# ConvFFN up and gate as seven block products instead of eight, and the down projection as a phase of its own

## The chip, the cores and the metric

The kernel runs on one core of a Trainium2 chip. The metric is the device time of one execution in microseconds. Its engines are TensorE (PE; PEld is its weight load), VectorE (DVE), ScalarE (ACT), GpSimd (POOL) and SyncE (SP), which issues nearly all transfers.

## The reference

One layer of a streaming encoder over 1024 prompt tokens and 32 sample tokens (1056 columns), in float32. Three mixers come first and are not touched. The part that changes is the ConvFFN (D_MODEL 1024, D_FF 2816):

```python
x = x + jnp.einsum('ble,ed->bld', jnp.concatenate([y_a, y_b, y_c], axis=-1), w_out)

h2 = _rmsnorm(x, norm_ffn_g)
up, gate = jnp.split(jnp.einsum('bld,df->blf', h2, w_up), 2, axis=-1)
g_conv, new_f = _causal_dwconv(gate, st_f, conv_ffn_w)
x = x + jnp.einsum('blf,fd->bld', jax.nn.silu(g_conv) * up, w_down)
```

Then a final RMSNorm. The convolution has 3 taps along the tokens; the last 2 gate inputs of each stream are outputs too.

## The kernel before, in words

Features lie on the 128 partitions and tokens along the columns, in three chunks `CH` of 256, 384 and 416. Each product is float32 by three matmuls (`three`, L245 to L250): weights and activations are split into a rounded part and its remainder (hi and lo, H and L), and hi·H, hi·L and lo·H are summed in PSUM. `convert` splits a weight block of 128x1024 with one ScalarE copy (L205) and one VectorE subtraction (L200); `weights` loads and converts a block or two ahead.

`o2`, the second half of the output projection, makes the residual stream `res` and the operands `fH`, `fL` of the ConvFFN in its evacuation `e_o2` (L1165 to L1176); behind its last block `rms_factor` (L1022 to L1024) makes the factor `rf` of each token, chunk by chunk. The ConvFFN runs over 22 feature blocks f in 11 pairs. For each f, `up_group` does the gate (8 row blocks x 3 chunks x 3 matmuls), its convolution and silu (L285, L290, L1203, L1205) and the up product, whose evacuation (L1211) multiplies; `mH` and `mL` (L1218, L1219) are the middle row in two parts and stay on chip. `down_group` adds the products of the pair before (8 output blocks x 3 chunks) into `res` (L1236 to L1240). The last two pairs go together, by chunks, with the last norm (`final`, `final_half`) among them. GpSimd does only `put_state` and `take_state` there (L475 to L483). No order is written out by hand: the order within an engine comes from a scheduler at build time, and each engine works through its own row of instructions in that order, waiting at each for what it needs.

## Time and profile before

| | us |
|---|---|
| median of 3 runs (1555.2 to 1558.69) | 1556.51 |
| span of the profiled execution | 1557.1 |
| PE busy in it | 1532.8 |
| DVE / ACT / POOL busy in it | 970.5 / 467.5 / 88.3 |
| from the first matmul of the ConvFFN (774.98) to the end | 782.1 |

A page of the profile lists busy time by engine, the chain of work that ended last, and the costliest groups of instructions. A matmul's own duration contains the pipeline; what each costs in a row of them is the distance of their starts.

### The profile page before, as it was taken

What the parts mean: (1) busy time and instruction counts of PE and PEld (TensorE: products, weight loads), DVE (VectorE), ACT (ScalarE), POOL (GpSimd) and SP (SyncE); (2) the same over time, 40 slices, a digit from 0 to 9 for tenths busy, and PEclk for the clock granted to TensorE, in tenths of its full rate; (3) what the DMA queues carried; (4) which work ended last, traced back from release to release, by engine and by line L of the source; (5) the groups of instructions that cost most, each with busy time, mean ns of one, the idle gap of its engine ahead of it and who ended that gap; (6) DMA issues with size and microseconds to landing.
All of it is one profiled execution on the core that took longest, in us unless ns stands there. A gap on an engine that the chain in (4) does not pass through costs nothing.

```text
span 1557.1 us, 23101 instructions
## 1 busy us (share of the span) xinstructions
PE 1532.8 (98%) x9677; PEld 1502.3 (96%) x9677; DVE 970.5 (62%) x1397; ACT 467.5 (30%) x754; POOL 88.3 (6%) x213
## 2 busy tenths in 40 slices
...
PEclk9999999999999999999999999999999999999999
...
GB/s 175 205 28 109 16 55 45 79 41 41 87 114 100 138 221 187 163 188 55 70 40 41 55 41 41 55 41 55 41 41 41 55 41 55 41 41 55 41 15 112
DMA packets 156758, 119.42 MB, mean 77 GB/s; under 512 B 9045, under 2 KB 145135, under 8 KB 156655
## 3 DMA queue, kind: packets, MB, share of 16 engines
...
q14 instruction: 27, 0.22, 0.0%
q10 hardware_dynamic: 16, 0.00, 0.0%
...
## 4 chain that ended last, share of the span: by engine, by line
PE 62%; DMA 1%; DVE 0%; ACT 0%; issue 0%; POOL 0%; SPq 0%; DVEq 0%; ACTq 0%; POOLq 0%
PE g L250 12%; PE g L245 12%; PE g L249 12%; PE g L1238 4%; PE g L1236 4%; PE g L1237 4%; PE xT L250 3%; PE xT L249 3%; PE xT L245 3%; PE xT L1236 1%; PE xT L1238 1%; PE xT L1237 1%; DMA zr<-zd 0%; DMA E<-acd 0%; PE yd L893 0%; PE st L883 0%
## 5 line engine op out<-in xcount | busy, mean ns | idle before, releaser
L245 PE MATMUL g<-hH,hi 128*128 128x416 f32 (+2 forms) x952 | 309.7, 325 | 0.0
L250 PE MATMUL g<-hH,lo 128*128 128x416 f32 (+2 forms) x952 | 307.3, 323 | 0.0
L249 PE MATMUL g<-hL,hi 128*128 128x416 f32 (+2 forms) x952 | 307.3, 323 | 0.0
L249 PE MATMUL g<-fL,hi 128*128 128x384 f32 (+2 forms) x792 | 255.9, 323 | 0.0
L250 PE MATMUL g<-fH,lo 128*128 128x384 f32 (+2 forms) x792 | 255.6, 323 | 0.0
L245 PE MATMUL g<-fH,hi 128*128 128x384 f32 (+2 forms) x792 | 255.6, 323 | 0.0
L245 PEld LDWEIGHTS g<-hH,hi 128*128 128x128 f32 x952 | 179.8, 189 | 1.8 <-issue 1.2
L249 PEld LDWEIGHTS g<-hL,hi 128*128 128x128 f32 x952 | 179.8, 189 | 0.4
L250 PEld LDWEIGHTS g<-hH,lo 128*128 128x128 f32 x952 | 179.6, 189 | 0.5 <-DVE lo L200 0.2
L290 DVE SCALAR_TENSOR_TENSOR cacc<-cb,par,cacc 128x1086 f32<-128x1086 f32 (+1 forms) x120 | 159.2, 1327 | 7.3 <-ACT cacc L287 5.7
L200 DVE TENSOR_TENSOR lo<-raw,hi 128x1024 fp32r<-128x1024 f32 x122 | 149.2, 1223 | 21.0 <-ACT hi L205 20.9
L249 PEld LDWEIGHTS g<-fL,hi 128*128 128x128 f32 x792 | 149.4, 189 | 0.4 <-issue 0.2
L250 PEld LDWEIGHTS g<-fH,lo 128*128 128x128 f32 x792 | 149.4, 189 | 0.5 <-issue 0.2
L245 PEld LDWEIGHTS g<-fH,hi 128*128 128x128 f32 x792 | 149.4, 189 | 0.3
L285 ACT ACTIVATE ca<-gb,par 128x1058 f32<-128x1058 f32 x22 | 26.0, 1182 | 407.8 <-DVE gb L1198 407.8
L1240 DVE TENSOR_TENSOR res<-res,g 128x416 f32<-128x416 f32 (+2 forms) x186 | 96.2, 522 | 60.7 <-PE g L1238 54.4
L1236 PE MATMUL g<-mH,hi 128*128 128x384 f32 (+2 forms) x396 | 129.0, 326 | 0.0
L1238 PE MATMUL g<-mH,lo 128*128 128x384 f32 (+2 forms) x396 | 128.5, 324 | 0.0
L1237 PE MATMUL g<-mL,hi 128*128 128x384 f32 (+2 forms) x396 | 128.0, 323 | 0.0
L205 ACT ACTIVATE hi<-raw 128x1024 fp32r<-128x1024 f32 x121 | 124.3, 1046 | 11.4 <-DMA raw<-in_w_in_dram 6.7
L1198 DVE TENSOR_TENSOR gb<-g,rf 128x384 f32<-128x384 f32 (+2 forms) x77 | 29.7, 410 | 142.4 <-PE g L250 142.4
L250 PE MATMUL xT<-fH,lo 128*128 128x256 f32 (+2 forms) x264 | 85.1, 323 | 0.0
...
## 6 DMA issues: line engine op xcount, KB each, us to landing
...
```

What stands on the lines that cost most here:

```text
L200: v.tensor_tensor(out=lo, in0=r, in1=hi.bitcast(F32), op=ALU.subtract)
L205: act.activation(hi, r, AF.Copy)
L245: pe.matmul(o, hi[:, k, :], x, start=first, stop=False)
L249: pe.matmul(o, hi[:, k, :], y, start=False, stop=False)
L250: pe.matmul(o, lo[:, k, :], x, start=False, stop=last)
L285: act.activation(out[:, u:u + n], buf[:, b:b + n], AF.Copy, scale=w_of(0))
L290: v.scalar_tensor_tensor(out=out[:, u:u + n], in0=buf[:, b + j:b + j + n], scalar=w_of(j), in1=out[:, u:u + n], op0=ALU.mult, op1=ALU.add)
L1198: v.tensor_tensor(out=buf[:, b:b + n], in0=ps[:, o:o + n], in1=rf[:, c0 + o:c0 + o + n], op=ALU.mult)
L1236: pe.matmul(o, hi[:, m, :], a[:, c0:c0 + w], start=(f == some[0]), stop=False)
L1237: pe.matmul(o, hi[:, m, :], b[:, c0:c0 + w], start=False, stop=False)
L1238: pe.matmul(o, lo[:, m, :], a[:, c0:c0 + w], start=False, stop=(f == some[-1]))
L1240: v.tensor_tensor(out=rc, in0=rc, in1=o, op=ALU.add)
```

## The change

Up and gate of one f, with the tokens halved (528 columns) and the 1024 input rows halved, are a 2 x 2 block product. One level of Strassen's scheme replaces its 8 block products by 7 (P1, P5, P6, P2, P7, P3, P4 in this order), each of 4 row blocks and two runs of 264 columns. Its operands are sums of weight halves (`make_sums`, on GpSimd), split again into two parts for each product (`make_w`), and sums of activation halves (`make_x`), made once at the start out of `rows` (the normalized residual before its factor), and split too (`split_x`). Sums of products are made in PSUM where a bank can go on, else in the evacuations (`after`): ScalarE copies P1, P5 and P2 out, GpSimd adds P1 and P5, VectorE adds for P6, P7, P3 and P4, and GpSimd multiplies by `rf`. `finish` does the convolution, the silu and the product, and writes the middle row to DRAM (`midd`). The residual stream is written to DRAM (`r2d`) by the evacuation of `o2`, and is loaded again for down.

The down projection comes after all f. For two halves h of the outputs and three chunks it adds over all 22 f in four PSUM banks: the same 1584 matmuls of 256, 384 and 416 columns as before. `next_wd` loads and splits down weights (in the first and third chunk of h = 0), `next_mid` loads and splits 128 rows of a chunk's middle from DRAM, both four f ahead. All of PSUM is one pool of eight banks. `up_group`, `down_group`, `fH`, `fL` and the resident `res` go; their removed lines are those of the kernel above and are not repeated:

```diff
+            x = rows[m] = slot(T, name=f"row{m}")
...
+            def e_o2(j, c0, w, ps, m=m, r=r, x=x):
...
-                act.activation(a[:, c0:c0 + w], rc, AF.Copy, scale=gk)
-                v.scalar_tensor_tensor(out=b[:, c0:c0 + w], in0=rc, scalar=gk,
-                                       in1=a[:, c0:c0 + w].bitcast(F32), op0=ALU.mult, op1=ALU.subtract)
+                act.activation(x[:, c0:c0 + w], rc, AF.Copy, scale=pcol(at["gf"] + m))
...
+                if j == 2:
+                    deferred.append(lambda: dma(out=r2d[m], in_=r))
...
+        def split_x(i, k, src):
+            q = (xpool.tile([P, T], F32R, name=f"X{i}{k}") if i == "P1" else slot(T, F32R, name=f"X{i}{k}"))
+            X[i, k] = q
+            act.activation(q[:, 0:H], src, AF.Copy)
+            v.tensor_tensor(out=q[:, H:T], in0=src, in1=q[:, 0:H].bitcast(F32), op=ALU.subtract)
+        def make_x(i, k):
+            a, b = rows[k], rows[k + 4]
+            b11, b12, b21, b22 = a[:, 0:H], a[:, H:T], b[:, 0:H], b[:, H:T]
+            if i == "P5":
+                t = xt_[k, 0] = slot(T, name="xt12")
+                pool.tensor_tensor(out=t[:, 0:H], in0=b12, in1=b11, op=ALU.subtract)
+                v.tensor_tensor(out=t[:, H:T], in0=b22, in1=t[:, 0:H], op=ALU.subtract)
+            if i == "P7":
+                t = xt_[k, 1] = slot(T, name="xt34")
+                pool.tensor_tensor(out=t[:, 0:H], in0=b22, in1=b12, op=ALU.subtract)
+                v.tensor_tensor(out=t[:, H:T], in0=b21, in1=xt_[k, 0][:, H:T], op=ALU.subtract)
+            src = {"P1": b11, "P2": b21, "P3": b22}.get(i)
+            if src is None:
+                n, h = {"P5": (0, 0), "P6": (0, 1), "P7": (1, 0), "P4": (1, 1)}[i]
+                src = xt_[k, n][:, h * H:h * H + H]
+            split_x(i, k, src)
+        raws, sums, wops = {}, {}, {}
...
+        def make_sums(f):
...
+            u, g = raws[f]
+            a, b = slot(1024, name="s12"), slot(1024, name="s34")
+            pool.tensor_tensor(out=a[:, 0:512], in0=g[:, 0:512], in1=g[:, 512:1024], op=ALU.add)
+            pool.tensor_tensor(out=a[:, 512:1024], in0=a[:, 0:512], in1=u[:, 0:512], op=ALU.subtract)
+            pool.tensor_tensor(out=b[:, 0:512], in0=u[:, 0:512], in1=g[:, 0:512], op=ALU.subtract)
+            pool.tensor_tensor(out=b[:, 512:1024], in0=u[:, 512:1024], in1=a[:, 512:1024], op=ALU.subtract)
+            sums[f] = (a, b)
...
+        def make_w(f, i):
...
+            n, h = {"P1": (0, 0), "P2": (0, 1), "P4": (1, 1), "P5": (2, 0), "P6": (2, 1), "P7": (3, 0),
+                    "P3": (3, 1)}[i]
+            src = (*raws[f], *sums[f])[n][:, 512 * h:512 * h + 512]
+            w = wops[f, i] = slot(1024, F32R, name="wop")
+            act.activation(w[:, 0:512], src, AF.Copy)
+            v.tensor_tensor(out=w[:, 512:1024], in0=src, in1=w[:, 0:512].bitcast(F32), op=ALU.subtract)
...
+            def product(self, i):
+                b = {"P1": "B", "P2": "B", "P5": "D", "P3": "D"}.get(i, "A")
+                new = i in ("P1", "P5", "P6")
+                w = wops.pop((self.f, i))
+                for c, (c0, n) in enumerate(C2):
+                    if new:
+                        self.banks[b, c] = bank()
+                    o = self.banks[b, c][:, 0:n]
+                    for k in range(4):
+                        hi, lo = w[:, k * P:k * P + P], w[:, 512 + k * P:512 + k * P + P]
+                        x = X[i, k]
+                        xh, xl = x[:, c0:c0 + n], x[:, H + c0:H + c0 + n]
+                        kw = {"skip_group_check": not new}
+                        pe.matmul(o, hi, xh, start=(new and k == 0), stop=False, **kw)
+                        pe.matmul(o, hi, xl, start=False, stop=False, **kw)
+                        pe.matmul(o, lo, xh, start=False, stop=(k == 3), **kw)
+                    self.after(i, c, c0, n, o)
...
+            def after(self, i, c, c0, n, o):
+                s1, s5 = self.s[:, c0:c0 + n], self.s[:, H + c0:H + c0 + n]
+                u2, s15 = self.t[:, c0:c0 + n], self.t[:, H + c0:H + c0 + n]
+                if i == "P1":
+                    act.activation(s1, o, AF.Copy)
+                elif i == "P5":
+                    act.activation(s5, o, AF.Copy)
+                    pool.tensor_tensor(out=s15, in0=s1, in1=s5, op=ALU.add)
+                elif i == "P6":
+                    v.tensor_tensor(out=u2, in0=o, in1=s1, op=ALU.add)
+                elif i == "P2":
+                    act.activation(self.u[:, c0:c0 + n], o, AF.Copy)
+                elif i == "P7":
+                    self.gate_to(H + c0, n, o, s15)
+                    if c == 1:
+                        pool.tensor_tensor(out=self.gb[:, 2 + H:2 + NP], in0=self.gb[:, 2 + H:2 + NP],
+                                           in1=rf[:, H:NP], op=ALU.mult)
+                        pool.tensor_tensor(out=self.gb[:, 4 + NP:4 + T], in0=self.gb[:, 4 + NP:4 + T],
+                                           in1=rf[:, NP:T], op=ALU.mult)
+                elif i == "P3":
+                    v.tensor_tensor(out=self.u[:, H + c0:H + c0 + n], in0=o, in1=u2, op=ALU.add)
+                    if c == 1:
+                        pool.tensor_tensor(out=self.u, in0=self.u, in1=rf, op=ALU.mult)
+                else:
+                    self.gate_to(c0, n, o, s1)
+                    if c == 1:
+                        pool.tensor_tensor(out=self.gb[:, 2:2 + H], in0=self.gb[:, 2:2 + H], in1=rf[:, 0:H],
+                                           op=ALU.mult)
+                        self.finish()
+            def finish(self):
+                f, gb, u = self.f, self.gb, self.u
+                take_state(fpack, gb, 2, f)
...
+                for _ in conv_steps(ca, 2, lambda i: pcol(at["w_f"] + NF * i + f), whole(gb, 2)):
+                    pass
+                act.activation(ca, ca, AF.Silu)
+                for t, a, n in run_pieces(2):
+                    v.tensor_tensor(out=u[:, t:t + n], in0=ca[:, a:a + n], in1=u[:, t:t + n], op=ALU.mult)
+                dma(out=midd[f], in_=u)
...
+        load_up(0)
+        load_up(1)
+        make_sums(0)
+        for i in ORDER:
+            for k in range(4):
+                make_x(i, k)
+            if i in ORDER[:3]:
+                make_w(0, i)
+        rows.clear()
+        xt_.clear()
...
+        AHEADW = 3
+        for n, (f, i) in enumerate(steps):
+            if i == ORDER[0]:
+                unit = Unit(f)
+                put_state(unit.gb, 2, "st_f", f, NF)
+            if i == ORDER[2] and f + 1 < NF:
+                make_sums(f + 1)
+            if n + AHEADW < len(steps):
+                make_w(*steps[n + AHEADW])
+            unit.product(i)
+            if i == ORDER[4]:
+                raws.pop(f)
+                sums.pop(f)
+                load_up(f + 2)
...
+        w_jobs = iter([(h, f) for h in range(2) for f in range(NF)])
+        CORDER = ((0, 1, 2), (2, 1, 0))
+        m_jobs = iter([(h, j, f) for h in range(2) for j in CORDER[h] for f in range(NF)])
+        def next_wd():
+            for h, f in w_jobs:
+                r = slot(512, name="rawd")
+                dma(out=r, in_=w_down[0, f * P:(f + 1) * P, 512 * h:512 * h + 512])
+                w = wd[h, f] = slot(1024, F32R, name="wd")
+                act.activation(w[:, 0:512], r, AF.Copy)
+                v.tensor_tensor(out=w[:, 512:1024], in0=r, in1=w[:, 0:512].bitcast(F32), op=ALU.subtract)
+                return
...
+        def next_mid():
+            for h, j, f in m_jobs:
+                r = small("midr")
+                dma(out=r[:, 0:w], in_=midd[f][:, c0:c0 + w])
...
+        for _ in range(4):
+            next_wd()
+            next_mid()
+        for h in range(2):
+            for m in range(4 * h, 4 * h + 4):
+                load_res(m)
...
+            for n, j in enumerate(CORDER[h]):
+                c0, w = CH[j]
...
+                ps = [bank() for _ in range(4)]
+                for f in range(NF):
+                    if h == 0 and n != 1:
+                        next_wd()
+                    next_mid()
+                    q = wd[h, f]
+                    a, b = mids.pop((h, j, f))
+                    for m in range(4):
+                        o = ps[m][:, 0:w]
+                        hi, lo = q[:, m * P:m * P + P], q[:, 512 + m * P:512 + m * P + P]
+                        pe.matmul(o, hi, a[:, 0:w], start=(f == 0), stop=False)
+                        pe.matmul(o, hi, b[:, 0:w], start=False, stop=False)
+                        pe.matmul(o, lo, a[:, 0:w], start=False, stop=(f == NF - 1))
+                    if n == 2:
+                        del wd[h, f], q
+                for m in range(4):
+                    rc = res[4 * h + m][:, c0:c0 + w]
+                    v.tensor_tensor(out=rc, in0=rc, in1=ps[m][:, 0:w], op=ALU.add)
+                if h and j:
+                    final(j)
+        final_half(1)
```

TensorE at the end of o2. Before, the matmul for the root mean square of the last chunk (`misc`, which waits for VectorE) stands 40 matmuls into the gate of f = 0:

```order
L245 MATMUL g_7368<-fH5_6993,hi57_7213 128x384
L1022 MATMUL misc_7326<-ss2_6450,ones_71 128x416 [waits DVE_49]
L249 MATMUL g_7368<-fL5_6994,hi57_7213 128x384
L250 MATMUL g_7368<-fH5_6993,lo57_7214 128x384
L245 MATMUL g_7368<-fH6_7102,hi57_7213 128x384
```

Now:

```order
L233 MATMUL g_7264<-gH7_6430,lo56_7091 128x416
L1005 MATMUL misc_7296<-ss2_6455,ones_71 128x416 [waits DVE_49]
L1272 MATMUL g_7472<-XP10_7346,wop_7358 128x264
L1273 MATMUL g_7472<-XP10_7346,wop_7358 128x264
L1274 MATMUL g_7472<-XP10_7346,wop_7358 128x264
```

It stands directly behind the last matmul of o2 and ahead of all of P1.

VectorE at the same place, now (`ss2` is the sum that this matmul reads, `xt12` a sum of activation halves that waits for GpSimd, `XP5` and the like are operands, `wop` a weight operand):

```order
L1152 TENSOR_TENSOR o2_7289<-g_7264,rb_6434 128x416 [waits PE_49]
L1206 TENSOR_TENSOR xt12_7361<-row4_6879,xt12_7361 128x528 [waits Pool_49]
L1154 TENSOR_TENSOR r1_7087<-r1_7087,o2_7289 128x416 [waits DVE_49]
L1197 TENSOR_TENSOR XP50_7364<-xt12_7361,XP50_7364 128x528 [waits Activation_49]
L1206 TENSOR_TENSOR xt12_7367<-row5_6985,xt12_7367 128x528 [waits Pool_49]
L1161 TENSOR_TENSOR ss2_6455<-ss2_6455,o2q_7293 128x416 [waits Activation_49]
...
L1197 TENSOR_TENSOR XP42_7457<-xt34_7427,XP42_7457 128x528 [waits Activation_49]
L1197 TENSOR_TENSOR XP43_7460<-xt34_7433,XP43_7460 128x528 [waits Activation_49]
L1247 TENSOR_TENSOR wop_7469<-rawf_7332,wop_7469 128x512 [waits Activation_49]
```

`wop_7469` is the operand of P2 of f = 0; in VectorE's row it stands behind the operands of the products that come after P2.

GpSimd in one f of the loop. Before, it had four instructions in each f:

```order
L475 MEMSET gb_7331 128x2
L477 COPY gb_7331<-par_77 128x2
L482 COPY fpack_7330<-gb_7331 128x2
L483 COPY fpack_7330<-gb_7331 128x2
```

Now it has fourteen, of which these are the wide ones (`ps2` takes P1 + P5):

```order
L1289 TENSOR_TENSOR ps2_8434<-ps15_8433 128x264 [waits Activation_49]
L1233 TENSOR_TENSOR s12_8501<-rawf_8359 128x512 [waits DMAHW5_49]
L1235 TENSOR_TENSOR s34_8502<-rawf_8357,rawf_8359 128x512 [waits DMAHW4_49,PE_49]
L1234 TENSOR_TENSOR s12_8501<-s12_8501,rawf_8357 128x512 [waits Pool_49]
L1236 TENSOR_TENSOR s34_8502<-rawf_8357,s12_8501 128x512 [waits Pool_49]
L1289 TENSOR_TENSOR ps2_8434<-ps15_8433 128x264 [waits Activation_49]
L1297 TENSOR_TENSOR gb_8432<-gb_8432,rf_6456 128x496 [waits DVE_49]
...
L1304 TENSOR_TENSOR u_8431<-u_8431,rf_6456 128x1056 [waits DVE_49,Activation_49]
L1308 TENSOR_TENSOR gb_8432<-gb_8432,rf_6456 128x528 [waits DVE_49]
```

And VectorE there, from the product of the f before to the evacuations of P6 (`ps2` from `g`) and the operands ahead:

```order
L273 SCALAR_TENSOR_TENSOR ca_9149<-gb_8916,par_77,ca_9149 128x1058 [waits Activation_49]
L1247 TENSOR_TENSOR wop_9163<-rawf_8841,wop_9163 128x512 [waits Activation_49]
L273 SCALAR_TENSOR_TENSOR ca_9149<-gb_8916,par_77,ca_9149 128x1058 [waits DVE_49]
L1247 TENSOR_TENSOR wop_9194<-s34_8986,wop_9194 128x512 [waits Activation_49]
L1320 TENSOR_TENSOR u_8915<-ca_9149,u_8915 128x1024 [waits Activation_49]
L1320 TENSOR_TENSOR u_8915<-ca_9149,u_8915 128x32
L1247 TENSOR_TENSOR wop_9233<-s34_8986,wop_9233 128x512 [waits Activation_49]
L1291 TENSOR_TENSOR ps2_9160<-g_9236,ps15_9159 128x264 [waits PE_49]
L1247 TENSOR_TENSOR wop_9264<-rawf_8843,wop_9264 128x512 [waits DMAHW3_49,Activation_49]
L1291 TENSOR_TENSOR ps2_9160<-g_9250,ps15_9159 128x264 [waits PE_49]
```

Both evacuations of P6 stand behind the convolution and the product of the f before.

SyncE where the up products end and down begins, now (`mid21` is the write of the last middle row; `rawd` are down weights, here of f = 1 to 4, `res` the residual rows):

```order
L1364 DMA rawd_12789<-in_w_down_dram 128x512
L1374 DMA midr_12862<-mid5_7312 128x256 [waits DMAHW4_49,DVE_49]
L1364 DMA rawd_12800<-in_w_down_dram 128x512 [waits PE_49]
L1321 DMA mid21_7328<-u_12541 128x1056 [waits DMAHW3_49,DVE_49,Pool_49]
L1374 DMA midr_12885<-mid6_7313 128x256 [waits DMAHW5_49,DVE_49]
L1364 DMA rawd_12811<-in_w_down_dram 128x512 [waits PE_49]
...
L1386 DMA res0_12822<-r2d0_6447 128x1056 [waits PE_49]
...
L1386 DMA res3_12828<-r2d3_6450 128x1056 [waits DMAHW4_49,PE_49]
L1364 DMA rawd_12834<-in_w_down_dram 128x512 [waits DMAHW5_49,PE_49]
```

The write of `mid21`, which waits for the end of the last f's chain, stands ahead of the weights of f = 3, and the residual rows ahead of those of f = 4. Before, all loads of the ConvFFN are weight blocks (L177), one behind the other.

## Rows read from the trace of the kernel before

**Rows 1.** The page: the span, what each engine was busy in it (us, share, instructions), the chain of work that ended last by engine, and the slices of the granted TensorE clock (tenths, 40 slices).

```profile
span 1557.1 us, 23101 instructions
PE 1532.8 (98%) x9677; PEld 1502.3 (96%) x9677; DVE 970.5 (62%) x1397; ACT 467.5 (30%) x754; POOL 88.3 (6%) x213
PEclk9999999999999999999999999999999999999999
PE 62%; DMA 1%; DVE 0%; ACT 0%; issue 0%; POOL 0%; SPq 0%; DVEq 0%; ACTq 0%; POOLq 0%
```

**Rows 2.** Busy time of each engine in five stretches that cover the ConvFFN and the tail (us; instructions in brackets; then granted clock, DMA share, GB/s).

```profile
774.98:787.00 12.02, 12.02 (x74) 11.56 (x73) 8.14 (x8) 2.09 (x4) 0.00 (x0) 1.00 0.42 121
787.00:1041.00 254.00, 254.00 (x1582) 253.47 (x1581) 126.97 (x198) 49.00 (x47) 6.46 (x32) 1.00 0.15 44
1041.00:1500.00 459.00, 458.93 (x2847) 457.54 (x2846) 235.12 (x369) 87.25 (x86) 11.72 (x54) 1.00 0.15 46
1500.00:1541.99 41.99, 41.84 (x270) 40.74 (x269) 24.27 (x52) 11.53 (x36) 0.00 (x0) 1.00 0.18 67
1541.99:1557.10 15.11, 7.88 (x64) 7.27 (x62) 6.88 (x18) 3.88 (x10) 0.00 (x0) 0.83 0.28 105
```

**Rows 3.** TensorE in order of time (start, us, line, operation, shape): the first matmul of a run of 24 of 256 columns, the first of the 24 of 384 behind it the first of the 24 of 416 behind that, and the one after them, in o2; then the last matmul of o2, the first of the ConvFFN, and the matmuls of the last rms_factor among the gate's.

```profile
704.37 0.28 PE L245 MATMUL g<-gH,hi 128*128 128x256 f32 x1
...
707.24 0.34 PE L245 MATMUL g<-gH,hi 128*128 128x384 f32 x1
...
711.40 0.35 PE L245 MATMUL g<-gH,hi 128*128 128x416 f32 x1
...
715.92 0.28 PE L245 MATMUL g<-gH,hi 128*128 128x256 f32 x1
...
774.79 0.35 PE L250 MATMUL g<-gH,lo 128*128 128x416 f32 x1
774.98 0.28 PE L245 MATMUL g<-fH,hi 128*128 128x256 f32 x1
...
780.62 0.93 PE L1022 MATMUL misc<-ss,ones 128*128 128x416 f32 x2
```

**Rows 4.** Groups of VectorE's instructions from 775 to 1500 us by line and shape (count, busy us, mean ns of one, idle before).

```profile
L200 DVE TENSOR_TENSOR lo<-raw,hi 128x1024 fp32r<-128x1024 f32 x63 | 76.8, 1219 | 0.0
L290 DVE SCALAR_TENSOR_TENSOR ca<-gb,par,ca 128x1058 f32<-128x1058 f32 x44 | 58.0, 1319 | 29.3 <-ACT ca L285 29.3
L1205 DVE TENSOR_TENSOR ca<-ca,rf 128x1024 f32<-128x1024 f32 x22 | 27.0, 1226 | 14.1 <-ACT ca L1203 13.9
L1211 DVE TENSOR_TENSOR pf<-g,ca 128x256 f32<-128x256 f32 x11 | 4.7, 425 | 0.0
L1205 DVE TENSOR_TENSOR ca<-ca,rf 128x32 f32<-128x32 f32 x22 | 4.1, 186 | 0.0
```

**Rows 5.** Groups of GpSimd's instructions by line and shape, whole span (columns as in Rows 4).

```profile
L856 POOL TENSOR_TENSOR xe<-xd,dend 128x512 f32<-128x512 f32 x16 | 18.1, 1134 | 55.3 <-DVE xd L850 55.3
L477 POOL COPY gb<-par 128x2 f32<-128x2 f32 x22 | 11.7, 534 | 0.2 <-issue 0.2
L482 POOL COPY fpack<-gb 128x2 f32<-128x2 f32 x22 | 4.1, 188 | 649.9 <-DVE gb L1198 649.9
```

**Rows 6.** GpSimd and VectorE in order of time, at three places where both work at once (start, us, line, operation; L874 reads one operand from PSUM, the tile misc).

```profile
569.38 1.09 POOL L819 TENSOR_SCALAR_AFFINE_SELECT E<-E 128x1024 f32<-128x1024 f32 x1 [10.14 <-DMA E<-acd]
570.44 2.05 POOL L856 TENSOR_TENSOR xe<-xd,dend 128x512 f32<-128x512 f32 x1
...
605.20 1.05 POOL L856 TENSOR_TENSOR xe<-xd,dend 128x512 f32<-128x512 f32 x1 [3.31 <-DVE xd L850]
...
862.69 0.99 POOL L477 COPY gb<-par 128x2 f32<-128x2 f32 x1
```

```profile
569.48 2.10 DVE L1016 SCALAR_TENSOR_TENSOR gL<-xbc,par,gH 128x1056 fp32r<-128x1056 f32 x1
...
605.03 1.21 DVE L874 TENSOR_TENSOR E<-E,misc 128x1024 f32<-128x1024 f32 x1
606.16 1.31 DVE L1016 SCALAR_TENSOR_TENSOR gL<-xbc,par,gH 128x1056 fp32r<-128x1056 f32 x1
```

**Rows 7.** VectorE in order of time around the first matmul of the ConvFFN at 774.98.

```profile
775.18 0.59 DVE L1165 TENSOR_TENSOR o<-g,rb 128x416 f32<-128x416 f32 x1 [0.31 <-PE g L250]
775.68 2.54 DVE L1024 RECIPROCAL rf<-rf 128x384 f32<-128x384 f32 x1
778.14 0.53 DVE L1167 TENSOR_TENSOR res<-res,o 128x416 f32<-128x416 f32 x1
...
779.95 0.58 DVE L1176 TENSOR_TENSOR ss<-ss,o2q 128x416 f32<-128x416 f32 x1
782.24 2.75 DVE L1024 RECIPROCAL rf<-rf 128x416 f32<-128x416 f32 x1 [1.70 <-ACT rf L1023]
```

**Rows 8.** Busy time of each engine in three stretches of o1 (columns as in Rows 2).

```profile
640.00:644.00 4.00, 4.00 (x37) 2.81 (x36) 2.16 (x3) 0.00 (x0) 0.00 (x0) 1.00 0.99 280
644.00:648.00 4.00, 4.00 (x17) 4.00 (x17) 3.50 (x9) 0.00 (x0) 0.00 (x0) 0.57 0.13 43
648.00:652.00 4.00, 4.00 (x26) 3.96 (x25) 0.74 (x3) 1.55 (x2) 0.00 (x0) 1.00 0.17 33
...
664.00:668.00 4.00, 3.23 (x19) 2.89 (x17) 2.18 (x3) 1.15 (x2) 0.00 (x0) 1.00 0.98 323
```

**Rows 9.** The chain of work that ended last, in order of time (start, us, what): a load from DRAM, from its issue to its landing, and the first steps behind it.

```profile
658.57 6.92 DMA zr<-zd
665.52 1.09 ACT zr L998
666.67 1.14 issue
```

**Rows 10.** Groups of ScalarE's instructions from 775 to 1500 us (columns as in Rows 4).

```profile
L285 ACT ACTIVATE ca<-gb,par 128x1058 f32<-128x1058 f32 x22 | 26.0, 1182 | 407.8 <-DVE gb L1198 407.8
L1203 ACT ACTIVATE ca<-ca 128x1058 f32<-128x1058 f32 x22 | 24.0, 1089 | 51.0 <-DVE ca L290 51.0
L1168 ACT ACTIVATE fH<-res,par 128x416 fp32r<-128x416 f32 x1 | 0.6, 644 | 3.3 <-DVE res L1167 3.3
```

181 lines of the change are left out of this document (76 added, 105 removed).

## The prediction

> **What bounds the kernel now.** I read the page first: PE is busy 1532.8 of 1557.1 us, its clock is full in nearly every slice, and the chain that ended last names no engine but PE with more than a percent [rows 1]. Then the stretches of the ConvFFN: PE fills each of them until 1541.99, while DVE is busy about half, ACT a fifth and POOL under 3% [rows 2]. So the ConvFFN (774.98 to the end, 782.1 us) costs what its matmuls cost, and a change of it gains what it takes off PE, as long as nothing else makes PE wait. The third view is PE in order of time, for the price of a matmul: 24 of 256 columns start within 2.87 us (0.1196 each), 24 of 384 within 4.16 (0.1733), 24 of 416 within 4.52 (0.188) [rows 3]. That is 0.42 to 0.46 ns per column and no visible fixed part. A block of 264 columns, an estimate by this slope, costs 0.123.
>
> **Matmuls removed.** Before, up and gate of one f are 48 matmuls of each width: 48 x (0.1196 + 0.1733 + 0.188) = 23.1 us. Now they are 7 products x 24 matmuls x 0.123 = 20.66 us. Down keeps its 1584 matmuls (254 us). The gain is 2.44 x 22 = **-53.6 us**. That the weight loads (one for each matmul) still hide at 264 columns is shown by the 256-column row, so this term is sure to about 2 us. All else is what PE newly waits for.
>
> **The loop.** Per f the change adds to DVE seven weight subtractions of 512 columns instead of two of 1024; by the rows for 256 and 1024 [rows 4] each takes 0.69. With two convolution steps of 1.32 and the product of 1.22 + 0.19, DVE has 8.9 us of instructions that read both operands from SBUF; the nine evacuations that read PSUM (264 columns, about 0.43 each) add 3.9. ACT has 7 x 0.71 + 1.18 + 1.09 + six copies of about 0.5 = 10.3 us [rows 10], DMA about 1.6 MB per 20 us; both hide. POOL gets four sums of 512 columns, one multiplication of 1056, one of 528, one of 496 + 32, and two additions of 264. The only row of this kind is 1.04 us for 512 (alone; 1.134 on average) [rows 5, 6], so: 4.2 + 2.15 + 1.07 + 1.1 + 1.1, with the small copies about 10.5 us.
>
> Each engine alone would fit. But rows 6 show that they don't run at once: at 569.38 POOL works 1.09 us, DVE's subtraction is issued at 569.48 and takes 2.10 (1.31 at 606.16), and POOL's next, issued at 570.44, takes 2.05 (1.05 at 605.20). Each took the time that the other still held plus its own. A copy of two columns on POOL takes 0.99 where DVE is at work and 0.188 on its usual row [rows 5, 6]. Beside an L874, which reads one operand from PSUM, neither is stretched (605.03 and 605.20). So 8.9 + 10.5 = 19.4 us of each 20.66 go one behind the other, in the order asked.
>
> The Trainium skill has this as a rule (SBUF — State Buffer, Who interferes with whom): DVE and GpSimd share a pair of ports as an exclusive lock held for a whole instruction, and a DVE instruction with two SBUF inputs contends with a GpSimd instruction that reads SBUF. It speaks against sums on POOL here; by it the period is that of the next paragraph, without it 20.66, and the trace agrees with the rule.
>
> Does it reach PE? I follow one f from the last P4 matmul of the f before (t = 0), in DVE's own order, which front shows. P4's evacuation and POOL's multiplication by `rf` end at 1.7, ACT's first tap at 2.9, the first convolution step at 4.3, a weight part 5.0, the second step 6.3, a weight part behind POOL's addition 7.5, the product behind POOL's first sum (1.04) 9.8, its 32 columns behind the second sum 11.0, the next weight part behind the third 12.7, and only then the evacuation of P6's first half: 13.15. PE wants to start P7 into that same bank after P1, P5, P6 and P2, at 4 x 2.95 = 11.8. It waits 1.4, and 0.2 at the second half. The period is 22.3 instead of 20.66: 1.6 x 21 = **+34 us**. The bounds: with no turn-taking the evacuation ends at 10.0, and the cost is nothing; with POOL at its average of 1.134 for 1.04 the period is about 23.5, and the cost 60. I take 34, as 1.04 is what POOL takes when nothing holds it, and the waits are already counted.
>
> **Into up.** Before, o2 runs into the gate without a gap (774.79, 774.98), as `rms_factor`'s matmul lies among the gate's [rows 3]. Now it stands ahead of P1. The sum that it reads is in DVE's row behind two reciprocals (the 384 one takes 2.54) [rows 7] and two `xt12` that wait for POOL, which is behind `make_sums`: P1 starts some 13.6 us after o2 ends. Then P2's operand stands in DVE's row behind all operands of P2, P7, P3 and P4. From the end of o2 DVE must do 24 splits and 8 sums of 528 columns (0.71 each by rows 4, together 22.6), three weight parts (2.1), two reciprocals (5.3) and three evacuations (1.7): 31.7 us before P2's lo matmuls, nothing of it hidden but under P1, P5 and P6. POOL's 12 instructions of that start (4 x 1.04 and 8 x 1.07, 12.7 us) take turns with it, and a little of them lies ahead: 43. P2, P7, P3 and P4 take 11.8, so f = 0 ends 55 us after o2 instead of 20.66: **+34 us** (24 without turn-taking; 36 if none of POOL's lies ahead). After PE's only small matmuls before 644 the clock is 0.57 for 4 us [rows 8]; such a stretch behind this idle time costs about **+2** (0 to 4).
>
> **Into down.** SP's row has the last middle row's write ahead of the weights of f = 3, and four residual rows (2.16 MB) ahead of those of f = 4. That write waits for the last f's chain: multiplication, tap, two steps, silu, product (1.07 + 1.18 + 2.64 + 1.09 + 1.41, and evacuation and hand-overs, 8.6 us). At the 280 to 323 GB/s that full DMA queues reach [rows 8] the residual rows take 7 us more, the middle row 2; a transfer of one row with its queue took 6.92 from issue to landing [rows 9], of which I put 2 behind the others; ACT and DVE split for 1.4. So f = 4 ends near 21.5, where five f of 12 matmuls of 256 columns are 7.2 us of PE: **+15 us** (8 if the write is early, 22 with the queue's full latency). The rest of this chunk needs 393 KB per 1.435 us, 274 GB/s, just what DMA gives. A slow clock behind the wait, as above: **+3** (0 to 4).
>
> **The end.** The transposes of `final` for two chunks stand ahead of the next chunk's matmuls, and four evacuations end together: **+4** (0 to 9). All up to o1 is unchanged; in o2 DVE has one instruction less per chunk and four splits more, under PE.
>
> **The sum**, on the profiled execution's 1557.1 (0.6 above the median, which I take off again): -53.6 + 34 + 34 + 2 + 15 + 3 + 4 = +38.4. **Forecast 1595 us**; with its own bounds about 1572 to 1615.
>
> **Rivals.** *The lock doesn't reach PE* (chance 0.22): DVE and POOL interleave so that P6 is evacuated by 11.8. For it: a slack of 1.8 us in the order without turns, and an order where POOL asks late would keep it; against: 19.4 of 20.66 us on one pair. Then 0 for the loop, 24 for the start: 1556.5 - 53.6 + 24 + 2 + 15 + 3 + 4 = 1551, or 1541 with the lower bounds of the rest: faster. It decides where the stall per f falls under (53.6 - 48 - 3.1)/21 = 0.12 us. *Heavier contention* (0.13): POOL at 1.134 and more, period 23.5: 1621. *The arithmetic alone* (0.05): both changes of phase hide as well; for it speaks only that o2 hid its chain before; 1507, and with it the 264-column price is right. That the 7 products don't shorten PE's work is excluded by rows 3.
>
> **How the numbers follow.** The forecast has 0.60. 0.2% (3.1 us) is about what a measurement of this kernel can tell from no change: 1553.4 to 1559.6. Of the first rival's chance I put 0.16 below that and 0.06 inside; with the arithmetic alone, faster is 0.21, same 0.06, slower 0.73. The range, 1545 to 1622, holds the forecast, most of the first rival and the second one's centre.
>
> **What would show it.** Matmul starts 0.123 apart within a product; PE idle of 1.4 us before P7 in each f, released by DVE's L1291; POOL's L1233 to L1236 at up to twice 1.04, DVE's L1247 above 0.69; f's period 22.3; PE idle 13 us behind o2 and some 20 before P2 of f = 0; SP waiting for POOL or DVE at L1321 of f = 21, and PE idle near 14 us in the first five f of down. I am wrong if the period is 20.7, or if down waits for DMA all along.

## The result and the profile after

The changed kernel takes 1573.18 us (median of 4 runs, 1570.45 to 1577.39), the kernel before 1556.13: ratio 1.0112, interval 1.0094 to 1.0130. It is slower by 17 us where 38 were forecast. The profiled execution of the changed kernel is its slowest, with a span of 1575.7 us, 18.6 over [rows 1]; the table below accounts for these 18.6.

The page of the changed kernel: span, busy time, the granted clock in 40 slices, and the chain that ended last by engine.

```profile
span 1575.7 us, 25521 instructions
PE 1497.1 (95%) x10205; PEld 1454.9 (92%) x10205; DVE 1057.8 (67%) x1449; ACT 608.2 (39%) x1156; POOL 424.3 (27%) x441
PEclk9999999999999899999889999999999979999999
PE 81%; DVE 8%; DMA 3%; ACT 2%; POOL 2%; issue 2%; SPq 0%; POOLq 0%; DVEq 0%; ACTq 0%
```

PE is busy 36 us less than in [rows 1], and yet the span grew: the chain now runs through DVE, DMA, ACT and POOL for 15% of it. Three slices of the clock from 748 us on read 8, 8 and 7: two around the start of up, one at the start of down. The stretches (columns as in [rows 2]) show which engine PE waits beside:

```profile
770.60:783.40 12.80, 0.96 (x3) 0.52 (x3) 10.63 (x8) 5.13 (x9) 12.80 (x9) 0.69 0.11 44
783.40:820.00 36.60, 27.30 (x166) 25.91 (x165) 31.49 (x47) 16.93 (x33) 18.52 (x15) 0.78 0.10 29
820.00:1240.00 420.00, 412.12 (x3325) 404.68 (x3324) 315.98 (x393) 159.16 (x301) 304.63 (x276) 1.00 0.26 74
1240.00:1265.30 25.30, 25.30 (x211) 25.30 (x211) 13.33 (x25) 6.29 (x12) 11.54 (x15) 1.00 0.08 27
1265.30:1300.00 34.70, 18.64 (x100) 16.93 (x98) 14.55 (x27) 12.55 (x27) 1.50 (x2) 0.75 0.65 215
1300.00:1330.00 30.00, 20.71 (x145) 18.64 (x146) 12.43 (x22) 10.15 (x22) 0.00 (x0) 1.00 0.50 152
1330.00:1575.70 245.70, 236.39 (x1416) 233.49 (x1415) 100.54 (x196) 83.86 (x179) 0.00 (x0) 0.98 0.43 135
```

PE stands nearly still for 12.8 us behind o2, is held back for the 36.6 us of f = 0, loses a little all through the loop, and then for 65 us at the start of down, where neither DVE, ACT nor the DMA queues (share 0.65, then 0.50) are full. By term, from PE in order of time (starts of the first and last matmul of each stage; up's 22 x 168 matmuls take 20.34 us per f where nothing waits, 0.1211 each):

| term | forecast | profiled execution | how |
|---|---|---|---|
| up's matmuls | -53.6 | -60.7 | 22 x (20.34 - 23.1) |
| o2 | 0 | -4.5 | last matmul 770.34, before 774.79 [rows 3] |
| into up | +36 | +29.6 | 13.1 from there to P1 (before 0.2), f = 0 in 37.0 for 20.34 |
| loop, f = 1 to 21 | +34 | +17.7 | periods over 20.34 |
| into down | +18 | +36.3 | the first two chunks take 113.6 us, their 264 matmuls each 77.3 at the prices of [rows 3] |
| the rest and the end | +4 | +0.2 | |
| sum | +38.4 | +18.6 | |

**Into up.** TensorE in order of time, four of its waits; then two stretches, from P1 to the end of the last of these waits and from there to the end of f = 0:

```profile
782.53 1.75 PE L1005 MATMUL misc<-ss,ones 128*128 128x416 f32 x2 [11.84 <-DVE ss L1161]
...
802.52 0.45 PE L1272 MATMUL g<-XP,wop 128*128 128x264 f32 x1 [4.29 <-ACT ps L1286]
804.40 0.59 PE L1272 MATMUL g<-XP,wop 128*128 128x264 f32 x1 [0.77 <-ACT wop L1246]
807.16 0.59 PE L1274 MATMUL g<-XP,wop 128*128 128x264 f32 x1 [1.51 <-DVE wop L1247]
```

```profile
783.46:807.16 23.70, 14.40 (x83) 13.01 (x81) 23.70 (x34) 14.48 (x28) 6.00 (x5) 0.79 0.02 5
807.16:820.51 13.35, 13.35 (x88) 13.35 (x89) 7.73 (x14) 2.45 (x5) 12.98 (x11) 0.78 0.24 72
```

The first wait is that of the norm's matmul for the sum in VectorE's row, as forecast. The other three are P2's. It waits first for the copy of P1 out of the bank that both use, which stands in ScalarE's row behind operands that wait for VectorE, and then for the two parts of its weights. The last wait ends at 807.16, and up to there from P1 on VectorE is never idle (23.70 of 23.70 us). Behind it nothing waits, but the 88 matmuls that are left take 13.35 us where they need 10.7 at 0.1211 each: after PE had been busy 14.40 of 23.70 us they go 0.22 us apart at first, with a granted clock of 0.58 up to 814.00, mostly its lower level, and from there on at the full one.

**The loop.** VectorE, GpSimd and TensorE in order of time in f = 5 (period 22.03) and in f = 15 (20.90):

```profile
911.15 3.44 DVE L1320 TENSOR_TENSOR u<-ca,u 128x1024 f32<-128x1024 f32 x2
912.27 2.27 POOL L1235 TENSOR_TENSOR s<-rawf 128x512 f32<-128x512 f32 x1
914.50 1.29 POOL L1234 TENSOR_TENSOR s<-s,rawf 128x512 f32<-128x512 f32 x1
914.51 1.83 DVE L1247 TENSOR_TENSOR wop<-s,wop 128x512 fp32r<-128x512 f32 x1
916.26 0.42 DVE L1291 TENSOR_TENSOR ps<-g,ps 128x264 f32<-128x264 f32 x1
916.74 0.39 PE L1272 MATMUL g<-XP,wop 128*128 128x264 f32 x1 [1.19 <-DVE ps L1291]
...
1127.02 3.44 DVE L1320 TENSOR_TENSOR u<-ca,u 128x1024 f32<-128x1024 f32 x2
1128.13 2.28 POOL L1235 TENSOR_TENSOR s<-rawf 128x512 f32<-128x512 f32 x1
1130.38 1.83 POOL L1234 TENSOR_TENSOR s<-s,rawf 128x512 f32<-128x512 f32 x1
1130.39 0.68 DVE L1247 TENSOR_TENSOR wop<-s,wop 128x512 fp32r<-128x512 f32 x1
1130.99 0.42 DVE L1291 TENSOR_TENSOR ps<-g,ps 128x264 f32<-128x264 f32 x1
```

In both f the two engines ask within 0.01 us of each other when the sum L1235 ends. In the first GpSimd goes first (1.29), VectorE's operand takes 1.83, and P6's evacuation L1291 comes after P7 has begun to wait for it; in the second VectorE goes first and takes 0.68, GpSimd's sum the 1.83. One draw decides 1.15 us. It is the same in every f from 2 to 20: this subtraction takes 1.82 or 1.83 us in the six with the long period and 0.68 in the others. Of the 20 periods from f = 1, 6 are 22.03 to 22.06, 12 are 20.88 to 20.90, one is 21.11 and one 20.34. So the draw is not all: where VectorE goes first, PE still loses 0.56 us at the two halves of P7, and these twelve f make 6.7 of the loop's 17.7 us, the six others 10.3.

**Into down.** TensorE's waits ahead of the first chunk (f = 0) and ahead of its f = 4; TensorE and ScalarE in order of time further on in it; then what SP waited for from 1285 to 1324 (us in total, times, longest):

```profile
1270.45 0.58 PE L1470 MATMUL g<-mH,wd 128*128 128x256 f32 x1 [4.73 <-ACT wd L1366]
...
1288.41 0.58 PE L1470 MATMUL g<-mH,wd 128*128 128x256 f32 x1 [7.17 <-ACT wd L1366]
...
1297.74 0.39 PE L1470 MATMUL g<-mH,wd 128*128 128x256 f32 x1 [1.02 <-ACT wd L1366]
...
1299.17 0.28 PE L1472 MATMUL g<-mH,wd 128*128 128x256 f32 x1
1299.49 0.42 ACT L1377 ACTIVATE mH<-midr 128x256 fp32r<-128x256 f32 x1 [1.80 <-PE g L1472]
1299.82 0.61 ACT L1366 ACTIVATE wd<-rawd 128x512 fp32r<-128x512 f32 x1
1300.48 0.39 PE L1470 MATMUL g<-mH,wd 128*128 128x256 f32 x1 [1.02 <-ACT wd L1366]
```

```profile
SPq L1374 <- DVE mL L1378: 24.3, 12, 4.3
```

Up to the start of f = 5 (1291.23) 18.7 us are lost, for a forecast of 15 + 3, and the wait that ends last there is the one that was forecast, of f = 4 for the weights behind the residual rows: the write of the last middle row goes out 8.5 us after up's last matmul (forecast 8.6), and f = 4 starts at 23.2. The wait ahead of f = 0, for weights behind the output of the state in SP's row, was not forecast and lies under it. The other 17.6 us are lost behind f = 5, where nothing was forecast. There PE waits for `wd`; `wd` stands in ScalarE's row behind `mH` of a much later f (f = 13's ahead of f = 8's weights); `mH` waits for the last matmul of six f before, because its ring has six buffers; that is the f that PE has just ended. So one f goes round PE, `mH`, `wd`, PE, in 2.73 us where its matmuls take 1.43 (f = 6 to f = 15). SP waits in the same way for a buffer of the raw rows.

### The profile page after: what moved, and what is told of

It reads as the page before. It is cut to its first block, busy times and chain, and to the rows that moved or that the text cites. A ratio compares the mean times of both kernels' runs of the same rounds, so it can differ in the third digit from the quotient of the medians.

```text
span 1575.7 us, 25521 instructions
## 1 busy us (share of the span) xinstructions
PE 1497.1 (95%) x10205; PEld 1454.9 (92%) x10205; DVE 1057.8 (67%) x1449; ACT 608.2 (39%) x1156; POOL 424.3 (27%) x441
## 4 chain that ended last, share of the span: by engine, by line
PE 81%; DVE 8%; DMA 3%; ACT 2%; POOL 2%; issue 2%; SPq 0%; POOLq 0%; DVEq 0%; ACTq 0%
PE g L228 13%; PE g L233 13%; PE g L232 13%; PE g L1272 7%; PE g L1274 7%; PE g L1273 7%; PE g L1470 6%; PE g L1472 5%; PE g L1471 5%; DVE wop L1247 2%; DVE ca L273 2%; DVE u L1320 1%; DVE XP L1197 1%; PE yd L876 1%; ACT ca L268 1%
## 5 line engine op out<-in xcount | busy, mean ns | idle before, releaser
L1272 PE MATMUL g<-XP,wop 128*128 128x264 f32 x1232 | 356.8, 290 | 12.9 <-DVE ps L1291 7.4
L1274 PE MATMUL g<-XP,wop 128*128 128x264 f32 x1232 | 351.6, 286 | 4.2 <-DVE wop L1247 4.2
L1273 PE MATMUL g<-XP,wop 128*128 128x264 f32 x1232 | 352.4, 286 | 0.0
L1272 PEld LDWEIGHTS g<-XP,wop 128*128 128x128 f32 x1232 | 235.0, 191 | 21.2 <-DVE ps L1291 15.3
L1274 PEld LDWEIGHTS g<-XP,wop 128*128 128x128 f32 x1232 | 233.5, 190 | 4.8 <-DVE wop L1247 4.8
L1273 PEld LDWEIGHTS g<-XP,wop 128*128 128x128 f32 x1232 | 234.3, 190 | 0.4 <-issue 0.4
L1470 PE MATMUL g<-mH,wd 128*128 128x256 f32 (+2 forms) x528 | 173.4, 333 | 26.9 <-ACT wd L1366 24.2
L1471 PE MATMUL g<-mL,wd 128*128 128x384 f32 (+2 forms) x528 | 171.9, 329 | 0.0
L1472 PE MATMUL g<-mH,wd 128*128 128x384 f32 (+2 forms) x528 | 167.1, 329 | 0.5 <-DVE wd L1367 0.5
L1378 DVE TENSOR_TENSOR mL<-midr,mH 128x256 fp32r<-128x256 f32 (+2 forms) x132 | 68.7, 524 | 146.3 <-ACT mH L1377 146.0
L1470 PEld LDWEIGHTS g<-mH,wd 128*128 128x128 f32 x528 | 102.1, 194 | 31.9 <-ACT wd L1366 28.2
L1377 ACT ACTIVATE mH<-midr 128x256 fp32r<-128x256 f32 (+2 forms) x132 | 65.3, 497 | 171.4 <-PE g L1472 164.2
L1471 PEld LDWEIGHTS g<-mL,wd 128*128 128x128 f32 x528 | 102.2, 194 | 0.3
L1472 PEld LDWEIGHTS g<-mH,wd 128*128 128x128 f32 x528 | 99.1, 193 | 1.2 <-DVE wd L1367 0.8
```

The source lines that it names most:

```text
L1272: pe.matmul(o, hi, xh, start=(new and k == 0), stop=False, **kw)
L1273: pe.matmul(o, hi, xl, start=False, stop=False, **kw)
L1274: pe.matmul(o, lo, xh, start=False, stop=(k == 3), **kw)
L1377: act.activation(a[:, 0:w], r[:, 0:w], AF.Copy)
L1378: v.tensor_tensor(out=b[:, 0:w], in0=r[:, 0:w], in1=a[:, 0:w].bitcast(F32), op=ALU.subtract)
L1470: pe.matmul(o, hi, a[:, 0:w], start=(f == 0), stop=False)
```

## The experiments

All times are medians, and the ratios are to the kernel before, measured beside each. Stages come from PE in order of time of each profiled execution: *into up* is from o2's last matmul to P1, and f = 0's time, *loop* the sum of the periods over 20.34, *two chunks* from up's last matmul to the first of 416 columns. *Loop* is more than the idle time of PE that some expectations go by (11 us in the changed kernel, 5.3 in e13), since it has the slower matmuls behind each wait too.

| kernel | us (runs) | ratio [interval] | into up | loop | two chunks |
|---|---|---|---|---|---|
| changed | 1573.18 (4) | 1.0112 [1.0094, 1.0130] | 13.1 + 37.0 | 17.7 | 113.6 |
| e1 | 1552.37 (10) | 0.9979 [0.9970, 0.9989] | 9.6 + 33.0 | 0 | 113.5 |
| e2 | 1617.87 (4) | 1.0408 [1.0385, 1.0431] | 11.9 + 35.7 | 68.1 | 113.4 |
| e3 | 1576.83 (4) | 1.0127 [1.0110, 1.0144] | 11.9 + 36.7 | 17.6 | 118.7 |
| e4 | 1579.25 (4) | 1.0151 [1.0133, 1.0170] | 11.8 + 38.7 | 25.6 | 112.4 |
| e5 | 1615.32 (4) | 1.0377 [1.0360, 1.0394] | 11.9 + 36.0 | 24.8 | 114.7 |
| e6 | 1574.16 (4) | 1.0105 [1.0079, 1.0131] | 11.9 + 30.9 | 22.3 | 112.8 |
| e7 | 1587.70 (4) | 1.0201 [1.0186, 1.0217] | 11.9 + 36.7 | 27.7 | 113.4 |
| e8 | 1578.32 (4) | 1.0136 [1.0121, 1.0151] | 13.1 + 36.6 | 23.4 | 110.6 |
| e9 | 1579.61 (4) | 1.0157 [1.0141, 1.0174] | 11.9 + 35.7 | 13.7 | 121.5 |
| e10 | 1579.22 (4) | 1.0155 [1.0140, 1.0171] | 11.9 + 37.0 | 20.5 | 113.7 |
| e11 | 1577.09 (4) | 1.0139 [1.0112, 1.0166] | 11.8 + 36.0 | 15.6 | 112.8 |
| e12 | 1580.31 (4) | 1.0160 [1.0145, 1.0175] | 11.9 + 32.3 | 20.7 | 122.5 |
| e13 | 1568.99 (10) | 1.0075 [1.0055, 1.0095] | 11.9 + 37.0 | 11.9 | 98.1 |
| e14 | 1584.39 (4) | 1.0181 [1.0147, 1.0215] | 11.9 + 35.8 | 12.9 | 113.9 |
| e15 | 1564.58 (6) | 1.0044 [1.0025, 1.0064] | 11.9 + 31.0 | 22.1 | 98.5 |
| e16 | 1559.19 (10) | 1.0019 [1.0010, 1.0029] | 11.9 + 37.7 | 0 | 113.4 |
| e17 | 1546.09 (4) | 0.9934 [0.9918, 0.9951] | 11.9 + 37.5 | 0 | 99.2 |
| e18 | 1550.05 (4) | 0.9963 [0.9948, 0.9978] | 12.2 + 31.9 | 0 | 103.6 |

**Do the sums on GpSimd reach PE? e1 leaves them out, e2 doubles two of them.**

```
-  a, b = slot(1024, name="s12"), slot(1024, name="s34")
-  pool.tensor_tensor(...)              # four sums
+  a, b = u, g                          # e1
...
+  for _ in range(2):                   # e2, behind the four sums, from the second f's on
+      pool.tensor_tensor(out=waste[:, 0:512], in0=g[:, 0:512], in1=u[:, 0:512], op=ALU.add)
```

> The four sums of weight halves per f on GpSimd are left out: P5, P6, P7 and P3 use raw weight halves instead, so the outputs are not the layer's. All else stays, the order on VectorE nearly too: P6's evacuation still stands behind the convolution and the product of the f before. Theory (GpSimd and VectorE take turns at SBUF): 4.2 us of turns per f go; the evacuation of P6 comes ahead of P7 in every f, the six stalls of 1.15 us and the 0.2 us of the others go, and with a shorter start the whole is 7 to 14 us faster than the changed kernel (1559 to 1566). Rival (the order on VectorE alone makes P7 wait, GpSimd is beside the point): the stalls stay, within 2 us of 1573.

> Two more additions of 512 columns per f on GpSimd, whose result nobody reads, from f = 1 on. Theory (turns): VectorE's two-operand SBUF work and GpSimd's come to about 21.5 us per f, more than PE's 20.9, so P7 waits in every f: period 22 to 23.5, 23 to 55 us slower than the changed kernel (1596 to 1628). Rival (GpSimd is off the path, with 9 us free per f): within 3 us of 1573.

Without the sums the loop waits nowhere, and into up is 7.5 us shorter; with two more it loses 68. So what GpSimd does in the loop does reach PE. It doesn't yet say by which wait. e1 gained more than its theory said (1559 to 1566), as the twelve f with the shorter loss, too, lose nothing without the sums.

**Is down's start ScalarE's row? e3 splits the weights on GpSimd, e5 loads and splits the middle rows there.**

```
-  act.activation(w[:, 0:512], r, AF.Copy)                  # e3: these two
-  v.tensor_tensor(out=w[:, 512:1024], in0=r, ...)
+  pool.tensor_copy(w[:, 0:512], r)
+  pool.tensor_tensor(out=w[:, 512:1024], in0=r, ...)
...
-  dma(out=r[:, 0:w], in_=midd[f][:, c0:c0 + w])            # e5: this and the row's two parts
+  pool.dma_start(out=r[:, 0:w], in_=midd[f][:, c0:c0 + w])
```

> Down weights are split by GpSimd (both parts), which is idle there; nothing else changes. Theory (in ScalarE's row the split of the weights of f = 8 stands behind that of the middle row of f = 13, which waits for PE to be done with f = 7, so PE and ScalarE go in lockstep, 2.72 us per f instead of 1.44): the lockstep goes; what stays is the chain over SyncE's row (a middle row's load waits for a split, weights behind it), 1.5 to 2.3 us per f, 7 to 20 us faster than the changed kernel (1553 to 1566). Rival (the first chunk of down is bound by what DMA brings, 393 KB per f): still 2.7 per f, within 3 us of 1573.

> The middle rows' loads are issued by GpSimd and split by GpSimd in down; weights stay with SyncE, ScalarE and VectorE. So nothing that waits for PE through the ring of middle rows stands ahead of weights in any row. Theory (in the first chunk of down, rows hold weights behind middle rows, on ScalarE and on SyncE): its period falls from 2.72 us per f to 1.44 to 1.8, 14 to 22 us faster than the changed kernel (1551 to 1559). Rival (DMA can't bring 393 KB in 1.44 us, or its latency sets it): 2.4 to 2.7 per f, within 5 us of 1573.

Both took `wd` out of the row behind `mH` and neither gained: in e3 PE waits for `wd` on GpSimd, which needs 2.0 us per f (0.68 + 1.35) and gets its weights behind SP's waits for middle rows; in e5 GpSimd makes the middle rows (0.55 us per f of it the issue of the load), and the later chunks go at its pace, 2.57 us per f of 384 columns and 2.67 of 416, where the changed kernel takes 2.10 and 2.27. But e5's first chunk shows what the queues can move (columns as in [rows 2]):

```profile
1284.00:1310.00 26.00, 18.78 (x133) 18.53 (x133) 16.15 (x19) 13.77 (x23) 19.80 (x32) 0.80 1.03 400
```

400 GB/s, where the changed kernel moves 215 and 152 at this place: the transfers are not what holds it.

**The start: e4 makes the first operands product by product, e6 the first sums under o2.**

```
-  for i in ORDER:                                    # e4: all operands ahead of the first product
+  make_first(ORDER[0]); make_first(ORDER[1])         # then one product's ahead of each product
...
+  if m == 6:                                         # e6: in o2's loop, in place of behind it
+      load_up(0); load_up(1); make_sums(0)
```

> The activation operands of f = 0 are written in the code in the order in which the products come, two products ahead, instead of all ahead of the first product. Theory (P2 of f = 0 waits for its operand and for P1's evacuation, which stand behind operands that are not needed yet on VectorE and ScalarE): P2 starts about 8 us earlier; VectorE's total of the start stays, so f = 0 ends 4 to 10 us earlier (1563 to 1569). Rival (VectorE's total alone sets it, in whatever order): within 2 us of 1573.

> The loads of f = 0 and 1 and the four sums of f = 0 are written ahead of the last two blocks of o2. Theory (the start is long because GpSimd's sums and xt12 take turns with VectorE, and begin late, behind the load that SyncE issues after two writes of r2d): 5 us of GpSimd's work go under o2, P1 and P2 of f = 0 start 4 to 7 us earlier, 1566 to 1569. Rival (VectorE's own 32 us of operands set the start): within 2 us of 1573.

e4 gained nothing (f = 0 took 38.7 us for 37.0, and VectorE was busy 37.2 of them): VectorE's total, with the turns in it, bounds f = 0, as forecast, not its order. e6 made f = 0 some 6 us shorter, VectorE's busy time in it fell from 31.4 to 26.5 us, and the loop's draws took 4.6 of it back.

**Where else might the sums stand? e7 issues them two products later, e10 makes them on VectorE, e14 takes other work from GpSimd.**

```
-  if i == ORDER[2] and f + 1 < NF:
+  if i == ORDER[4] and f + 1 < NF:                             # e7
...
-  pool.tensor_tensor(...)                                      # e10: the four sums
+  (v if f else pool).tensor_tensor(...)
...
-  pool.tensor_tensor(out=self.u, in0=self.u, in1=rf, op=ALU.mult)              # e14
+  v.tensor_tensor(out=o, in0=ps[m][:, 0:w], in1=rf[:, c0:c0 + w], op=ALU.mult) # on down's sums
```

> The sums of f + 1 are written at P7 of f instead of P6, so GpSimd asks for SBUF for them later; nothing is left out. Theory (who asks first decides: in six f the first sums get in ahead of VectorE's product and weight part, and P6's evacuation is late): the 1.47 us gaps ahead of P7 go, 6 to 11 us faster than the changed kernel (1562 to 1567). Rival (19.4 of 20.9 us on one pair: the wait comes back elsewhere, in the multiplications by rf and the next convolution): within 3 us of 1573.

> The four sums of the weights (512 columns each) are made by VectorE for every f but the first. Theory (GpSimd and VectorE take turns, and the loop's 11 us of waits before P7 come from both together needing 19.4 us of 20.6): VectorE makes a sum of 512 in about 0.7 us where GpSimd takes 1.3 to 2.2, so the pair needs 17.5 to 18.5 us; the loop's waits fall to 0 to 6 us, the whole to 1560 to 1569. Rival (what counts is what stands ahead of P6's evacuation in VectorE's own row, which is longer now): the loop's waits stay at 11 us or grow to 30, the whole is 1573 to 1592.

> The token factor of the last norm is no longer multiplied onto each up row by GpSimd (1056 columns, about 2.4 us in each f); it is multiplied onto down's sums by VectorE, four more products per chunk. Theory (the loop's waits come from GpSimd and VectorE together being nearly full, 19.4 us of 20.6): with 17.0 the waits fall from 11 to 0 to 3 us; down loses 1 to 4 us at its chunks' ends; the whole is 1562 to 1571. Rival (the waits hang on what stands ahead of the evacuation in the rows at that place, not on the total): the waits stay between 7 and 19 us, the whole at 1572 to 1585.

In all three the wait before P7 behind L1291 is still there: in nearly every f in e7 (1.18 us) and in e10 (0.81), so without a draw, and e7's four times lie within 1.5 us. e14 speaks against my theory of a pair that is too full: with 2.4 us per f less for it the profiled execution still loses 12.9 us in the loop, the products on down's sums cost 5.7 us behind the first two chunks, and the median is 11 us above the changed kernel's. Its four times reach from 1578.48, the profiled one, to 1591.49; where the others lost more, no trace shows.

**Loads: e8 moves residual rows, the state and the last norm; e11 loads o2's residual rows eight ahead.**

```
-  for m in range(4 * h, 4 * h + 4): load_res(m)      # e8: the first four eight f into the chunk,
+  if h == 0 and n == 0 and f == 8: ...               # give_state one chunk, final 6 to 12 f later
...
-  if m < 7: load_r1(m + 1)                           # e11
+  for m in range(8): load_r1(m)                      # ahead of the loop
```

> Three places in down: the state outputs are written after the first chunk instead of ahead of the first weights; the residual rows of the first half are loaded at f = 8 instead of ahead of f = 4; the last norm of a chunk comes after six f of the next chunk. Theory (weights stand behind these in SyncE's row: 5 us ahead of f = 0 and 7 us ahead of f = 4; and the next chunk's banks wait for the norm, 8 us at two places): 10 to 17 us faster than the changed kernel (1556 to 1563). Rival (the lockstep in the first chunk, or DMA, takes the time back): 0 to 6 us faster.

> The second half of o2 loads its eight residual rows at its start, as the kernel before does, and not one ahead of its use. Theory (o2 ended 4.5 us earlier than in the kernel before because its rows come one by one, not in one burst at its start): o2 ends at 773 to 775 us in place of 770.5 and the whole is 1576 to 1580. Rival (it ended earlier because VectorE no longer makes the low parts of the residual rows in the evacuations): o2 ends at 770 to 771.5 and the whole stays at 1571 to 1577.

e8 gained 3.0 us in the two chunks and 3.4 behind them; the loop took 5.7, and o2 ended 1.9 later. (e8, and e18 below, also issue the first four loads of weights ahead of the first four middle rows.) In e11 o2 ended at 774.2, in the other kernels at 770.3 to 773.4, but by a new wait at 692.38 (1.45 us, for a low part on VectorE), and the residual rows were issued no earlier than 679.41. It does not settle why o2 ends earlier than before.

**Two rings into down: e9 takes the parts out of their ring of six, e13 the raw rows out of their ring of four, e12 combines e9 with edits seen above.**

```
-  a = mpool.tile([P, 416], F32R, tag="mH", name="mH")          # e9, and mL
+  ab = slot(T, F32R, name="mid"); a, b = ab[:, 0:416], ab[:, 528:944]
...
-  r = small("midr")                                            # e13
+  r = slot(T, name="midr")
...
+  # e12: e9, e6, e10, and final_half(0) at f == 12 of its chunk
```

> The two parts of a middle row lie in a slot of the common pool in place of the ring of six, so that in ScalarE's row the copies of the middle rows stand one or two f ahead of the weights' copies and no longer five, and none of them waits for a matmul of six f before. Theory (the lockstep PE, mH, wd, PE makes the period of 2.72 us in down's first chunk): the period falls to 1.4 to 1.9 us, the first chunk with the wait before it from 59.3 us to 35 to 48, the whole to 1549 to 1561, all else as it was. Rival (the transfers give 393 KB in no less than 2.7 us while weights and middle rows come over the same queue): the first chunk stays at 55 to 60 us and the whole at 1570 to 1577.

> Middle rows in slots, the first sums made under o2, the other sums on VectorE, and the first half of the last norm put twelve f into its chunk. If the causes found so far are all and do not touch each other: first chunk of down -12 to -24 us, start -4 to -6, loop -5 to -11, the wait before the last norm's chunk -4 to -6, together 1526 to 1549, faster than the kernel before. Rival (as in the runs so far each wait removed is given back half by the next one in the rows): 1549 to 1566.

> The raw middle rows that down loads lie in slots of the common pool in place of the ring of four that they share with other small tiles; the ring of six for their two parts stays. In ScalarE's row the copy of a middle row now stands one f behind the weights' copy. Theory (both rings bound the way into down, one by ScalarE's row, the other by SP's; the transfers gave some 300 GB/s when nothing held them, which is 393 KB in 1.3 us): the periods of 2.7 us in the first chunk fall to 1.4 to 1.9 us, the two first chunks together from 113.6 us to 85 to 100, the whole to 1545 to 1562. Rival (the transfers themselves take some 2.7 us for 393 KB when rows of 128 x 256 are cut out of wider ones): the two chunks stay at 105 to 120 us, the whole at 1567 to 1580.

e9 failed, and shows the second ring. ScalarE in order of time and what SP waited for, 1285 to 1336, in e9:

```profile
1307.68 0.63 ACT L1366 ACTIVATE wd<-rawd 128x512 fp32r<-128x512 f32 x1 [3.27 <-DMA rawd<-in_w_down_dram]
...
SPq L1374 <- DVE mid L1378: 35.7, 12, 7.1
```

ScalarE no longer waits for PE, but SP waits before each pair of raw rows until VectorE has read the rows four back, and the weights stand behind in its row. The two chunks took 121.5 us, and e12, which has this edit too, 122.5; with e10's sums on VectorE it also has e10's loop, and ends at 1580.31. With the ring of the raw rows gone (e13; TensorE in order of time, and the stretch 1285 to 1310) the period is the matmuls' own:

```profile
1292.16 0.28 PE L1471 MATMUL g<-mL,wd 128*128 128x256 f32 x1
...
1293.59 0.28 PE L1471 MATMUL g<-mL,wd 128*128 128x256 f32 x1
...
1285.00:1310.00 25.00, 25.00 (x203) 25.00 (x202) 15.14 (x30) 17.51 (x37) 0.00 (x0) 0.95 0.91 310
```

1.43 us per f, 310 GB/s, PE busy throughout. e13 kept the ring of six: with the raw rows' loads in another order, `mH` stands one f behind the weights and no longer five ahead. The two chunks took 98.1 us instead of 113.6, within the theory's range, and the profiled execution 1557.25. Of the 20.8 us left over the matmuls' 77.3, 17.5 lie up to the start of f = 5, where the changed kernel loses 18.7. The median is 1568.99, with times up to 1574, outside the theory's range for the whole: the loop again, as the next runs show.

**One wait or the pair? e16 moves P6 one product ahead; e15 and e17, e18 combine.**

```
-  ORDER = ("P1", "P5", "P6", "P2", "P7", "P3", "P4")
+  ORDER = ("P1", "P6", "P5", "P2", "P7", "P3", "P4")           # e16
...
+  # e15: e13, e14, e6, final_half(0) at f == 12;  e17: e16 and e13
+  # e18: e17, e6, residual rows at f == 8 and give_state one chunk later, as in e8
```

> Raw middle rows in slots, the factor after down, the first f's sums made under o2, and the first half of the last norm put twelve f into its chunk. If the parts add: -13 to -28 us for down, -8 to -11 for the loop, -4 to -6 for the start, -2 to -5 for the last norm, +2 to +4 for the products after down: 1528 to 1549, faster than the kernel before by 0.5 to 1.8 per cent. Rival (what one part gives the next wait takes): 1549 to 1570.

> The products' order is P1, P6, P5, P2, P7, P3, P4 in place of P1, P5, P6, P2, P7, P3, P4 (what P6 needs of the rows' differences is made with it). P6's banks are read by VectorE two products ahead of P7 and no longer one, and in VectorE's row the two evacuations stand ahead of u x ca and of two operands; GpSimd and VectorE do the same work. Theory A (one wait: P7 behind P6's evacuation): the gaps of 1.47 us vanish, the up products from P1 on take 468 to 474 us in place of 481.8, the timed executions no longer scatter over 7 us, the whole is 1558 to 1567. Theory B (the pair is full, whatever the order): as many gaps at another product, 476 to 495 us, the whole at 1569 to 1585.

> e16's order and e13's slots for the raw middle rows. By theory A for the loop, and the rings for the way into down: e13's profiled execution, which had only 5.3 us of waits in its loop, was 1557.3, so without them in any execution 1545 to 1556, no slower than the kernel before and with timed executions close together. By theory B: 1560 to 1575 with e13's scatter of 17 us.

> e17 with the first f's sums under o2, the residual rows of down loaded eight f into its first chunk, and the convolution's state sent out one chunk later. If these add as in e6 and e8: -4 to -6 us at the start, -3 to -8 before and in down's first chunk against e17: 1534 to 1552, faster than the kernel before. If they are given back: as e17 within 4 us.

The loop's stretch of e16, and VectorE in one f of it:

```profile
820.00:1240.00 420.00, 420.00 (x3473) 420.00 (x3472) 316.03 (x412) 162.76 (x313) 311.15 (x286) 1.00 0.26 76
...
1134.22 1.78 DVE L1247 TENSOR_TENSOR wop<-s,wop 128x512 fp32r<-128x512 f32 x1
1135.93 0.76 DVE L1291 TENSOR_TENSOR ps<-g,ps 128x264 f32<-128x264 f32 x2
1136.62 1.87 DVE L1320 TENSOR_TENSOR u<-ca,u 128x1024 f32<-128x1024 f32 x2
```

VectorE and GpSimd are as busy as in the changed kernel (316 and 311 us of 420, there 316 and 305), L1247 still takes 1.78, and PE waits nowhere: both evacuations of P6 now stand ahead of u x ca, and P7 asks for its banks one product later after them. Ten times lie within 3.3 us. Theory A held, with 464.5 us from P1 on where it said 468 to 474. The one edit gives P6's evacuations one more product of time and a place further ahead in VectorE's row; which of the two would do alone was not tried. e17 adds the ring's edit and has both gains: 1546.09, 0.66% faster than the kernel before (interval 0.49 to 0.82%). e15, without e16's order, kept 22.1 us in its loop. e18 lost to e17 by 4 us: it won 5.6 in f = 0, but PE then stood 13.1 us before down, 5.8 more than in e17. It waited for `mH` of f = 0, whose load e18 issues at 1253.69 behind the write of the last middle row (1252.80), while e17 issues it at 1250.28 ahead of that write (1256.72).

## Why the prediction was half right

- *Matmuls removed* held; its size was 7 us short. 168 matmuls of 264 columns take 20.34 us, 0.1211 each, where I had drawn 0.123 from the slope in [rows 3].
- *The loop* had the right wait (P7 behind P6's evacuation, behind instructions that take turns with GpSimd) and about twice its size: 34 forecast, 17.7 measured. It is 0.84 us per f, far over the 0.12 below which the first rival would have had it. The step that failed is that the turns go "in the order asked" to the same end in every f. Where they do, in six f, PE loses 1.7 us for 1.6 forecast. At the deciding place both engines ask at once, and in twelve f VectorE won and PE lost 0.56. e1, e2 and e16 show the chain: no sums, no wait; more sums, more wait; the same work with P6 read earlier, no wait. The turns of "19.4 of each 20.66" hold: the same subtraction takes 1.83 us behind GpSimd's sum and 0.68 ahead of it. The Trainium skill has these turns as a rule (SBUF — State Buffer, Who interferes with whom), and the trace agrees with it, by the 1.83 for 0.68. But a pair that full is not by itself a loss: e16 has it and loses nothing, e14 lightens it and still waits.
- *Into up* held, 6 us too long: 13.1 us for 13.6 to P1, and f = 0 ends 50 us after o2 for 55. The wait for P2's weights on VectorE ended 36.6 us after o2, where I had 43; the slow clock behind it cost 2.7 for my 2. e4 and e6 bear out VectorE's total, with the turns, as its cause. What I missed is P1's copy in ScalarE's row, which made P2 wait first; it stands behind the same operands.
- *Into down* failed in its second part. Up to f = 5 the path and the size were right (18.7 us for 15 + 3). The step that failed is that the rest of this chunk was put at nothing, as it needs "just what DMA gives": in the trace DMA has a share of 0.50 there, e5's queues move 400 GB/s, and 17.6 us more are lost, 36.3 for 18. Two rings and the rows of ScalarE and SP, which none of my steps looked at, make them: the order of the changed kernel had `mH` of f = 13 ahead of `wd` of f = 8, and I didn't read what that one waits for. e13 shows it for the ring of the raw rows, without which the period is 1.43 us. For the ring of the parts it is read from the rows: in the changed kernel ScalarE waits for it, in e9, without it, no more, but that edit alone gained nothing, and in e13 the ring is still there and costs nothing, with `mH` behind the weights.
- *o2* was put at nothing and gave 4.5 us. Before, four residual rows are loaded while o1 runs, the load of `zr` takes 6.92 us [rows 9], PE stands still near 667, and from 644 to 648 the granted clock is 0.57 [rows 8]. After, these loads come behind 676, and PE has neither:

```profile
644.00:648.00 4.00, 4.00 (x26) 3.96 (x26) 3.30 (x9) 0.59 (x2) 0.00 (x0) 1.00 0.24 95
664.00:668.00 4.00, 4.00 (x27) 3.98 (x27) 4.00 (x5) 2.87 (x4) 0.00 (x0) 1.00 0.68 217
```

  I read this from the traces; e11 failed to bring it back, so it is argued and not shown. Some of it is the execution: the profiled one is 1 us ahead already at a write of `r1d` near 604 (603.57, before 604.54), and the runs whose code is the same up to there end o2 anywhere from 770.3 to 773.1.
- *The end* is as before within the accounting, not 4 us longer.
- The sum came out 20 us too high. The errors of the loop (-16), of the matmuls, the start and o2 (-18 together) and of the end (-4) go one way, the error into down (+18) the other. That the time still lies in my range, and on the slower side, is in part luck: without the 17.6 us of the two rings, which I hadn't forecast, it would be near that of the kernel before.
- Two readings of the prediction were wrong without changing the sum: the copy that took 0.99 beside DVE is L477, whose mean is 0.534; the 0.188 is that of L482, another copy [rows 5]. And the bound without turn-taking is 23 by its own terms (31.7 + 11.8 - 20.66), not 24.

Open: that the executions of the changed kernel differ by 7 us, and e13's by 17, because the draws in the loop fall differently is inferred from e16 and e17, which have no such waits and spread over 3.3 and 2.2 us, and from e7, which waits in nearly every f and spreads over 1.5; only profiled executions show their periods.
